# Expert stage of a decoder layer: a fixed TensorE order with neighbouring pairs of experts interleaved

## The chip, the cores and the metric

The kernel runs on one core of a Trainium2 chip, as one program. The metric is the device time in microseconds (us) from one launch, lower is better. All data are float32 in HBM; weights alone are about 460 MB, of which the experts' are 403 MB.

## The reference

One decoder layer over 256 tokens of width 1024: a token-mixing part with four gated branches, a layer norm, then a sparse expert layer and a second norm. The change concerns the expert layer (cut to what matters; `EXPERT_BLOCK` padding left out):

```
logits = h @ w_router + b_router                # 32 experts
top_v, top_e = top_k(logits, 4); gates = softmax(top_v)
for each expert e, for its tokens xb:
    hdn = xb @ w_up[e] + b_up[e]                # 1024 -> 2048
    glu = min(hdn[..., ::2], 7); lin = clip(hdn[..., 1::2], -7, 7)
    act = glu * sigmoid(1.702 * glu) * (lin + 1)
    y[token] += gate * (act @ w_down[e] + b_down[e])   # 1024 -> 1024
h = layer_norm(alpha * h + y)
```

Every expert is used by some tokens, so all of w_up (8.39 MB an expert) and w_down (4.19 MB) is read once.

## The kernel before

**Slabs and the stream of weights.** SBUF is an arena of 25 slabs, each 128 partitions by 2048 floats (1 MB). Weights and working buffers take slabs from it. All weight pieces stand in one list in the order of their use (`specs`); `load_one` (L267) takes a slab and issues the next load on SP's queue, and `pump(reserve)` issues loads while more than `reserve` slabs are free. A slab is reused when its last reader has ended, so a load waits in SP's queue for the engine that last used its slab. In the expert stage two slabs are kept free (`RES_MOE`), and nine from the last but one pair on (`RES_OVER`), for the overflow pass. A piece of w_up is 128 rows of 2048 floats: one 8 KB row for each partition. A piece of w_down is 256 rows of 1024 floats, as two 4 KB rows for each partition, row `p` and row `128 + p` (`rows`).

**Pairs of experts.** The experts are taken two at a time, in 16 pairs (`for e0`, L1592). Each expert has 64 places for tokens. `gather` (L1355 to L1364) builds the selection of the two experts' tokens on VectorE and GpSimd, multiplies the 256 tokens by it on TensorE into two PSUM tiles (pxs, L1360), and ScalarE writes the 8 pieces of transposed rows with the norm's gain and offset (L1364). `pair` (L1398) then does:

- the up product: 8 chunks of rows k, each with two slabs (one an expert); for each of four column blocks nb and both experts one matmul of 128 rows, 64 columns of the array and 512 values (L1416) into one of four PSUM tiles hp. The two experts of a pair use different halves of the array's columns. The biases are added by a matmul (L1410);
- `places`: the transposed selection and the gates of the places (L1437, L1439), copied by ScalarE (L1441);
- `hidden`: the activation of each of the four column blocks, one operation on ScalarE (L1424) and four on VectorE (L1423 to L1427), and two transposes on TensorE (pta, L1429), copied back by ScalarE (L1515);
- the down product: 4 chunks of two slabs, 8 matmuls each (L1447) into two PSUM tiles dp;
- in the third pair (`RESID`), the scaled residual, the output biases and the largest count of tokens of any expert (`residual`, L1368);
- `scatter`: the result times the gates in two float32r parts (ScalarE L1452, VectorE L1453), back to the tokens by matmuls (psc, L1456, L1457), added to the sum of all pairs on VectorE (L1463).

**The last pair** has its weights cut by columns, in the order `LAST`, so that w_up's blocks and w_down's halves alternate; these pieces have rows of 2 KB. Its result is added to the sum in PSUM (yf, L1478), and the second norm follows (L1618 on).

**The overflow pass.** An expert with more than 64 tokens would need a second pass. `overflow` (L1543) reads the largest count into a register of every engine (L1545) and branches around the pass (L1546); with these inputs the pass is not run. It stands ahead of the last pair. Behind it two loads go to ScalarE's queue (`OTHER`).

**What sets the order.** Within a dependency order, a scheduler of the language orders each engine's instructions by its own estimates of costs. The kernel writes the matmuls of a chunk with the experts alternating; the scheduler may move them. It also decides where the next pair's gather or the residual's matmuls stand among the others.

PSUM has 8 banks: four of tag pp (hp, yf), two of pt (pxs, psg, pta, psc and others), two of pd (dp).

Of the kernel before, what the change touches and what calls it, by code (L numbers as in the profile page):

```python
# [23 lines left out]
T = 256  # L24
# [31 lines left out]
OTHER = 2  # L56
ROWS_AT = 3
RES_OVER = 9
# [86 lines left out]
class Part:  # L145
    """A piece of a block that is freed as a whole."""
# [28 lines left out]
def tile_trunk(ctx, tc, a, out):  # L175
# [71 lines left out]
    # The last pair's weights come in an order that leaves little to do when the last of them is there: w_up by blocks  # L247
    # of columns, w_down by halves of its columns, the chunks of the first half as soon as their rows can be used.
# [64 lines left out]
            # ScalarE rounds; VectorE, and GpSimd for the last quarter, take the rest  # L313
# [20 lines left out]
    class Half:  # L334
        """Half of the columns of a tile that was split as a whole."""
# [31 lines left out]
    class X:  # L367
        """An activation [128, k, T] in two float32r parts."""
# [5 lines left out]
        def split(self, sl, src, hi_src=None, eng=None):  # L374
            """src: float32 on SBUF or PSUM"""
# [47 lines left out]
    class Moments:  # L423
        """Mean and reciprocal deviation over D, by halves."""
# [61 lines left out]
    # small parameters of the scan  # L486
# [115 lines left out]
        # a - 1 = expm1(x) cos(t) - 2 sin^2(t/2) + i a_im; divided by lam  # L602
# [41 lines left out]
        # the same with the halves exchanged: [im; re]  # L644
# [10 lines left out]
    def turn(dst, src, sine, sign):  # L655
        """The sine's part of a rotation of the pairs [re; im]: the halves change places."""
# [4 lines left out]
    def scan_part(m):  # L661
        """S5: the tables of eight groups, then V, the scan over chunks, and the outputs."""
# [6 lines left out]
        # E[state, g, k, n] = a^k b_bar ; Cp[state, g, k, n] = c a^(k+1)  # L669
# [15 lines left out]
        # taps k[n', (tau, n)] with seven zero taps before them, laid out in DRAM  # L685
# [61 lines left out]
    def scan_in():  # L747
        """S5 inputs by chunks of eight steps, the latest step first."""
# [19 lines left out]
    def scan_out():  # L768
# [17 lines left out]
        # gelu, tanh form  # L786
# [13 lines left out]
    def select():  # L800
        """Indexer scores and the best 64 keys of every query."""
# [39 lines left out]
    def sparse():  # L841
        """Attention over the selected latents."""
# [61 lines left out]
    def memory():  # L904
        """Attention over the memory."""
# [38 lines left out]
    # -- main stream: one weight tile after the other ------------------------  # L944
# [13 lines left out]
    def main():  # L958
# [21 lines left out]
        # residual in token layout  # L980
# [11 lines left out]
        # indexer and latents  # L992
# [60 lines left out]
        # convolution  # L1053
# [26 lines left out]
        # gates and branches: twice the merged value, transposed  # L1080
# [57 lines left out]
    def rows_in():  # L1138
        """Parameters of the experts: b_up in two stacked float32r parts, b_down and the norms' rows below it."""
# [17 lines left out]
    def route_in():  # L1157
        """The router's weights times the norm's gain, their sums, and what the norm's offset adds to the bias."""
# [82 lines left out]
    # -- output projection, first norm, router, by blocks of 128 tokens --------  # L1241
    # The router's product is taken before the norm: its gain rides on the weights, mean and deviation on the result.
# [58 lines left out]
    for b in range(2):  # L1301
# [20 lines left out]
        # places from 1 on, 0 for an expert that is not chosen  # L1322
# [5 lines left out]
    def gates():  # L1328
# [21 lines left out]
    def gather(sl):  # L1350
        """Rows of two experts, transposed; sl: their slots, [128, 2, 2]."""
        S2, xs = B(128, 2, 2, CAP), B(128, KC, 2 * CAP)
        for b in range(2):
            for e in range(2):
                (V if b else G).tensor_scalar(S2.ap[:, b, e, :], slot_i, sl[:, b, e:e + 1], None, op0=OP.is_equal)  # L1355
        p = [PT("pxs") for _ in range(2)]
        for b in range(2):
            for k in range(KC):
                # one flag for the groups of a bank
                PE.matmul(p[k // 4][:, k % 4 * 128:(k % 4 + 1) * 128], hN.ap[:, b, k * 128:(k + 1) * 128],  # L1360
                          S2.ap[:, b].rearrange("p e s -> p (e s)"), start=b == 0 and k % 4 == 0, stop=b == 1,
                          skip_group_check=True)
        for k in range(KC):
            S.activation(xs.ap[:, k, :], p[k // 4][:, k % 4 * 128:(k % 4 + 1) * 128], AF.Identity, bias=col(3, k),  # L1364
                         scale=col(2, k))
        return xs, S2

    def residual():  # L1368
        """The scaled residual and the output biases; the largest count."""
# [28 lines left out]
    def pair(xs, S2, gt, up_k, dn_k, pick, mid=None, first=False, last=None):  # L1398
# [20 lines left out]
        def hidden(nb, p):  # L1419
            """The activation of a block, transposed."""  # L1420
            hv = hp[nb].rearrange("p (f two) -> p f two", two=2)
            g, l, t = B(128, 256), B(128, 256), B(128, 256)
            V.tensor_scalar(g.ap, hv[:, :, 0], LIMIT, None, op0=OP.min)  # L1423
            S.activation(t.ap, g.ap, AF.Tanh, scale=0.5 * SWA)  # L1424
            V.tensor_scalar(l.ap, hv[:, :, 1], LIMIT, -LIMIT, op0=OP.min, op1=OP.max)
            V.scalar_tensor_tensor(l.ap, l.ap, 1.0, g.ap, op0=OP.add, op1=OP.mult)
            V.scalar_tensor_tensor(l.ap, t.ap, 1.0, l.ap, op0=OP.add, op1=OP.mult)  # L1427
            for j in range(2):
                PE.transpose(p[:, j * 128:(j + 1) * 128], l.ap[:, j * 128:(j + 1) * 128], ident)  # L1429
# [3 lines left out]
        def places():  # L1433
            """The transposed selection and the half gates of the slots."""
# [15 lines left out]
        def scatter(nb):  # L1450
            sl = slice(nb * 512, (nb + 1) * 512)
            S.activation(r_(yh.ap[:, sl]), dp[nb], AF.Copy, scale=gs_)  # L1452
            V.scalar_tensor_tensor(r_(yl.ap[:, sl]), dp[nb], gs_, yh.ap[:, sl], op0=OP.mult, op1=OP.subtract)  # L1453
            for b in range(2):
# [10 lines left out]
        if last:  # L1465
# [3 lines left out]
            yh, yl = R(128, D), R(128, D)  # L1469
            for what, j, k0, kn in LAST:  # L1470
# [4 lines left out]
                if what == DOWN and k0 == 0:  # L1475
# [17 lines left out]
                if what == DOWN and k0 + kn == KC:  # L1493
                    scatter(j)
        else:
# [13 lines left out]
            aT, ST = B(128, KC, 128), R(128, 2, 128)  # L1509
            gs_ = places()  # L1510
            for n2 in range(2):
                p = PT("pta")
                for i in range(2):
                    hidden(2 * n2 + i, p[:, i * 256:(i + 1) * 256])
                S.copy(aT.ap[:, n2 * 4:n2 * 4 + 4, :].rearrange("p k c -> p (k c)"), p)  # L1515
            dp = [PD(f"dp{i}") for i in range(2)]
            for k2 in range(KC // 2):
                with dn_k(k2) as wd:
                    for i, nb, e in ((i, nb, e) for i in range(2) for nb in range(2) for e in range(2)):
                        down(nb, 2 * k2 + i, e, wd[e][:, i, nb * 512:(nb + 1) * 512])  # L1520
            if mid:
# [4 lines left out]
            for nb in range(2):  # L1526
                scatter(nb)
        for t in (aT, ST, yh, yl):
            t.free()
# [13 lines left out]
    def overflow():  # L1543
        """Tokens past an expert's first 64."""
        cnt = nc.values_load(cnt_i[0:1, 0:1], min_val=0, max_val=T)  # L1545
        with tc.If(cnt > CAP):  # L1546
# [26 lines left out]
            with tc.For_i(0, T // CAP - 1, 1):  # L1573
                V.tensor_scalar(far, far, -float(CAP), None, op0=OP.add)
                with tc.For_i(0, NE, 2) as e0:
# [3 lines left out]
                    xs, S2 = gather(sl.ap)  # L1579
                    pair(xs.ap, S2.ap, gt.ap,  # L1580
# [67 lines left out]
```

## Time and profile before

| what | value |
|---|---|
| median of 3 runs | 1433.44 us (1432.83 to 1434.91) |
| span of the profiled execution | 1434.6 us |
| mean granted TensorE clock | 0.964 |
| bytes read by the weight queue | 454.80 MB in 133520 packets |
| loads of w_up on SP's queue | 255 of 1024 KB, 9.9 us from issue to landing |
| loads of w_down on SP's queue | 123 of 1024 KB (9.3 us) and 9 of 512 KB (7.3 us) |
| first expert matmul | 409.5 us |

How to read the lines: `L1416` is a line of the kernel; `PE` is a TensorE matmul, `PEld` its weight load, `DVE` VectorE, `ACT` ScalarE, `POOL` GpSimd, and a `q` behind a name means the engine's instruction queue (`SPq` issues loads). `hp<-slab,slab x112` means 112 such records that write tile hp. A float32 matmul has two records. In brackets stands the idle time before, and what ended it.

### The profile page before, as it was taken

How to read it: one execution, taken by the hardware profiler on the slowest of the kernel's cores; microseconds unless marked ns; L12 is line 12 of the kernel's file. 1: busy time of each engine (PE TensorE's matmuls, PEld its weight loads, DVE VectorE, ACT ScalarE, POOL GpSimd, SP SyncE). 2: the span in 40 equal slices, each digit the busy share in tenths (PEclk: the TensorE clock that was granted, in tenths of full speed). 3: DMA queues.
4: the chain of work that ended last, by engine and by line, in shares of the span. 5: the costliest groups of instructions: out<-in, count | busy, mean ns of one | idle time of the engine just before them, and what ended most of it. 6: DMA issues, size and time to landing. Idle time of an engine off the chain costs nothing. (4 is left out here: it accounts for less than half of the span.)

```text
span 1434.6 us, 17340 instructions
## 1 busy us (share of the span) xinstructions
PE 1332.6 (93%) x6936; PEld 722.8 (50%) x6936; DVE 472.4 (33%) x972; ACT 315.0 (22%) x600; POOL 162.7 (11%) x190
## 2 busy tenths in 40 slices
PE   8898889999999999999999999999999999999896
PEld 8697889899953343334243343434333343433332
DVE  5797935755623113311203111120211112021113
ACT  5553333654322010101101010110101011010101
POOL 3124341446210000000000000000000000000000
PEclk9899988999999999999999999999999999999898
DMA  9524155884799999699999999999999999999390
GB/s 262 216 63 129 60 158 177 267 322 181 292 347 418 384 423 427 262 427 398 396 394 410 395 398 427 398 395 402 390 405 380 426 394 426 399 401 385 119 336 30
DMA packets 137046, 463.38 MB, mean 323 GB/s; under 512 B 19352, under 2 KB 54240, under 8 KB 105952
## 3 DMA queue, kind: packets, MB, share of 16 engines
q1 hardware_dynamic: 133520, 454.80, 80.2%
q0 software_dynamic: 2608, 5.83, 1.6%
q10 hardware_dynamic: 832, 1.58, 0.3%
q8 instruction: 57, 0.93, 0.2%
q14 instruction: 29, 0.24, 0.0%
HBM read 459.09 MB, written 3.08 MB: 322 GB/s over the span
## 5 line engine op out<-in xcount | busy, mean ns | idle before, releaser
L1416 PE MATMUL hp<-slab,slab 128*64 128x512 f32 x2048 | 524.1, 599 | 0.0
L1416 PEld LDWEIGHTS hp<-slab,slab 128*64 128x64 f32 x2048 | 179.4, 137 | 309.8 <-issue 307.4
L1447 PE MATMUL dp<-slab,slab 128*64 128x512 f32 x1024 | 266.0, 625 | 10.1 <-ACT slab L1515 10.1
L1447 PEld LDWEIGHTS dp<-slab,slab 128*64 128x64 f32 x1024 | 77.3, 142 | 158.6 <-issue 141.8
L323 DVE TENSOR_TENSOR slab<-slab,slab 128x1024 fp32r<-128x1024 f32 (+1 forms) x90 | 105.1, 1178 | 60.3 <-ACT slab L318 54.5
L1355 POOL TENSOR_SCALAR slab<-slot_i,slot 128x64 f32<-128x64 f32 x32 | 14.0, 452 | 942.1 <-PE psg L1439 780.1
L318 ACT CAST slab<-slab 128x1024 fp32r<-128x1024 f32 x90 | 92.7, 1049 | 69.5 <-issue 13.6
L323 POOL TENSOR_TENSOR slab<-slab,slab 128x256 fp32r<-128x256 f32 (+1 forms) x58 | 90.6, 1567 | 149.0 <-ACT slab L318 123.2
L1441 ACT CAST slab<-psg 128x256 fp32r<-128x256 f32 x16 | 6.0, 373 | 357.5 <-PE hp L1410 354.9
L384 PE MATMUL pg<-slab,slab 128*128 128x256 f32 x256 | 75.4, 295 | 0.0
L386 PE MATMUL pg<-slab,slab 128*128 128x256 f32 x256 | 75.4, 294 | 0.0
L1355 DVE TENSOR_SCALAR slab<-slot_i,slot 128x64 f32<-128x64 f32 x32 | 7.0, 254 | 205.1 <-PE psg L1439 198.0
L385 PE MATMUL pg<-slab,slab 128*128 128x256 f32 x256 | 74.4, 291 | 0.0
L1360 PE MATMUL pxs<-slab,slab 128*128 128x128 f32 x512 | 63.6, 284 | 5.7 <-DVE slab L1463 4.3
L1364 ACT ACTIVATE slab<-pxs,pcol 128x128 f32<-128x128 f32 x128 | 46.5, 468 | 102.3 <-PE pxs L1360 102.3
L1360 PEld LDWEIGHTS pxs<-slab,slab 128*128 128x128 f32 x512 | 60.6, 197 | 12.1 <-issue 10.3
L1423 DVE TENSOR_SCALAR slab<-hp 128x256 f32<-128x256 f32 x64 | 26.8, 419 | 98.1 <-PE hp L1416 90.9
L1424 ACT ACTIVATE slab<-slab 128x256 f32<-128x256 f32 x64 | 26.7, 417 | 140.1 <-DVE slab L1423 140.1
L1429 PE MATMUL pta<-ident,slab 128*128 128x128 f32 x128 | 29.8, 316 | 24.4 <-DVE slab L1427 23.0
L384 PEld LDWEIGHTS pg<-slab,slab 128*128 128x128 f32 x256 | 50.6, 198 | 1.9 <-issue 1.4
L386 PEld LDWEIGHTS pg<-slab,slab 128*128 128x128 f32 x256 | 50.7, 198 | 0.9 <-issue 0.9
L385 PEld LDWEIGHTS pg<-slab,slab 128*128 128x128 f32 x256 | 50.6, 198 | 0.9 <-issue 0.9
(449 smaller groups left out, 1592.7 us busy)
## 6 DMA issues: line engine op xcount, KB each, us to landing
slab<-in_w_up_dram SPq DMA_DIRECT2D x255, 1024.0 KB, 9.9
slab<-in_w_down_dram SPq DMA_DIRECT2D x123, 1024.0 KB, 9.3
slab<-in_w_in_dram SPq DMA_DIRECT2D x29, 1024.0 KB, 6.2
slab<-in_w_branch_dram SPq DMA_DIRECT2D x8, 1024.0 KB, 6.3
slab<-in_w_down_dram SPq DMA_DIRECT2D x9, 512.0 KB, 7.3
slab<-in_w_mem_kv_dram SPq DMA_DIRECT2D x4, 1024.0 KB, 11.2
slab<-in_w_o_dram SPq DMA_DIRECT2D x4, 1024.0 KB, 7.1
slab<-kp_d POOLq DMA_DIRECT2D x32, 64.0 KB, 3.3
```

The source lines that it names most:

```text
L318: ins = S.copy(r_(hi[:, sl]), src[:, sl])
L323: ins = eng.tensor_tensor(r_(lo[:, p0:p1]), src[:, p0:p1], hi[:, p0:p1], op=OP.subtract)
L384: PE.matmul(dst, lh, rh, start=first, stop=False)
L385: PE.matmul(dst, lh, rl, start=False, stop=False)
L386: PE.matmul(dst, ll, rh, start=False, stop=last)
L1360: PE.matmul(p[k // 4][:, k % 4 * 128:(k % 4 + 1) * 128], hN.ap[:, b, k * 128:(k + 1) * 128], S2.ap[:, b].rearrange("p e s -> p (e s)"), st ...
L1364: S.activation(xs.ap[:, k, :], p[k // 4][:, k % 4 * 128:(k % 4 + 1) * 128], AF.Identity, bias=col(3, k), scale=col(2, k))
L1416: PE.matmul(hp[nb][e * 64:(e + 1) * 64, :], xs[:, k, e * CAP:(e + 1) * CAP], w, start=start, stop=k == KC - 1, skip_group_check=True)
L1423: V.tensor_scalar(g.ap, hv[:, :, 0], LIMIT, None, op0=OP.min)
L1424: S.activation(t.ap, g.ap, AF.Tanh, scale=0.5 * SWA)
L1429: PE.transpose(p[:, j * 128:(j + 1) * 128], l.ap[:, j * 128:(j + 1) * 128], ident)
L1447: PE.matmul(dp[nb][e * 64:(e + 1) * 64, :], aT.ap[:, k, e * 64:(e + 1) * 64], w, start=k == 0, stop=k == KC - 1, skip_group_check=True)
```

## The change

1. **A fixed order on TensorE.** The expert stage stands in `manual_schedule` for TensorE: its instructions run in the order in which the kernel writes them. The other engines' are ordered by the scheduler as before. In each chunk the two experts' matmuls alternate.
2. **Neighbouring pairs interleaved.** The gather of the next pair begins with the pair (selection), its matmuls are split into two halves, behind the chunk before the last and behind the last of the up product. `places` moves behind chunk 3 (`PLACES_AT`). The first two blocks of `hidden` stand ahead of the down product, the third and fourth behind its first and second chunk. The scaling by the gates (`shares`) stays at the end of a pair, but the matmuls of the scatter are returned as a function (`add`) and run behind the first chunk of the next pair's up product (`behind`).
3. **w_down by two rows a partition.** A piece of 256 rows is laid out with rows `2p` and `2p + 1` in partition p, one run of 8 KB. `hidden` therefore takes the activation's columns in another order (`p (q i two) -> p i q two`), in the overflow pass in the old one.
4. **The overflow pass inside the last pair**, ahead of the third piece of w_down's first half (`OVER_AT`). The reservation of nine slabs and the two loads on ScalarE's queue go.

The rest of the difference is comments. The core of the diff:

```diff
-OTHER = 2
+OVER_AT = (0, 4)
+PLACES_AT = 3
-RES_OVER = 9
...
-            specs.append((src.rearrange("(i p) c -> p i c", p=128), (i, src.shape[1])))
+            specs.append((src.rearrange("(p i) c -> p i c", p=128), (i, src.shape[1])))
...
+    class Gather:
...
+        def half(self, h):
+            p = PT("pxs")
+            for b in range(2):
+                for i in range(4):
+                    k = 4 * h + i
+                    PE.matmul(p[:, i * 128:(i + 1) * 128], hN.ap[:, b, k * 128:(k + 1) * 128],
+                              self.S2.ap[:, b].rearrange("p e s -> p (e s)"), start=b == 0 and i == 0, stop=b == 1,
+                              skip_group_check=True)
+            for i in range(4):
+                k = 4 * h + i
+                S.activation(self.xs.ap[:, k, :], p[:, i * 128:(i + 1) * 128], AF.Identity, bias=col(3, k),
+                             scale=col(2, k))
...
         def hidden(nb, p):
-            hv = hp[nb].rearrange("p (f two) -> p f two", two=2)
-            g, l, t = B(128, 256), B(128, 256), B(128, 256)
+            hv = hp[nb].rearrange("p (q i two) -> p i q two", i=2, two=2) if paired else \
+                hp[nb].rearrange("p (i q two) -> p i q two", i=2, two=2)
+            g, l, t = B(128, 2, 128), B(128, 2, 128), B(128, 2, 128)
...
         if last:
...
+            behind()
             for what, j, k0, kn in LAST:
...
+                if what == DOWN and (j, k0) == OVER_AT:
+                    over()
-                if what == DOWN and k0 == 0:
+                if what == DOWN and (j, k0) in (OVER_AT, (1, 0)):
                     for b in range(2):
                         last[b].y[j] = P("yf")
...
                 if what == DOWN and k0 + kn == KC:
+                    shares(j)
                     scatter(j)
...
         else:
...
+                if k == 0 and behind:
+                    behind()
+                if k == PLACES_AT:
+                    aT, ST = B(128, KC, 128), R(128, 2, 128)
+                    gs_ = places()
+                if k == KC - 2 and ahead_:
+                    ahead_.half(0)
+            if ahead_:
+                ahead_.half(1)
+            ga.free()
+            for nb in range(2):
+                p = PT("pta")
+                hidden(nb, p)
+                S.copy(aT.ap[:, 2 * nb:2 * nb + 2, :].rearrange("p k c -> p (k c)"), p[:, :256])
...
             for k2 in range(KC // 2):
                 with dn_k(k2) as wd:
                     for i, nb, e in ((i, nb, e) for i in range(2) for nb in range(2) for e in range(2)):
                         down(nb, 2 * k2 + i, e, wd[e][:, i, nb * 512:(nb + 1) * 512])
+                if k2 < 2:
+                    nb = 2 + k2
+                    p = PT("pta")
+                    hidden(nb, p)
+                    S.copy(aT.ap[:, 2 * nb:2 * nb + 2, :].rearrange("p k c -> p (k c)"), p[:, :256])
...
+            for nb in range(2):
+                shares(nb)
+
+            def add():
+                for nb in range(2):
+                    scatter(nb)
+                for t in (ST, yh, yl):
+                    t.free()
+            return add
...
-    for e0 in range(0, NE, 2):
-        final = e0 == NE - 2
-        if e0 == NE - 4:
-            st["spare"] = RES_OVER
-        if final:
-            overflow()
-            st["spare"] = RES_MOE
-        xs, S2 = gather(slot[:, :, e0:e0 + 2])
...
-            for _ in range(OTHER):
-                tc.keep_in_program_order(load_one(nc.scalar))
...
+    ga, behind = Gather(slot[:, :, 0:2]).all(), None
+    gates()
+    with tc.manual_schedule(engines={mybir.EngineType.PE}):
+        for e0 in range(0, NE, 2):
+            final = e0 == NE - 2
+            after = None if final else Gather(slot[:, :, e0 + 2:e0 + 4])
...
+            behind = pair(ga, gh[:, :, e0:e0 + 2],
...
+                          residual if e0 == RESID else None, e0 == 0, ln2 if final else None, after, behind, not final,
+                          overflow)
+            ga = after
```

More of the change, by code (lines that the diff above doesn't have):

```diff
@@ L1348, in vec_row, with __init__, all, free @@
         return p
[L1350 to L1366, printed above, removed]
+    class Gather:
+        def __init__(self, sl):
+            self.S2, self.xs = B(128, 2, 2, CAP), B(128, KC, 2 * CAP)
+            for b in range(2):
+                for e in range(2):
+                    (V if b else G).tensor_scalar(self.S2.ap[:, b, e, :], slot_i, sl[:, b, e:e + 1], None,
+                                                  op0=OP.is_equal)
+        def half(self, h):
+            p = PT("pxs")
+            for b in range(2):
+                for i in range(4):
[7 more added lines that the diff above has]
+                             scale=col(2, k))
+        def all(self):
+            for h in range(2):
+                self.half(h)
+            return self
+        def free(self):
+            for t in (self.xs, self.S2):
+                t.free()
     def residual():
@@ L1396, in residual, with pair @@
         V.tensor_copy(cnt_i, cf)
-    def pair(xs, S2, gt, up_k, dn_k, pick, mid=None, first=False, last=None):
+    def pair(ga, gt, up_k, dn_k, pick, mid=None, first=False, last=None, ahead_=None, behind=None, paired=True,
+             over=None):
+        xs, S2 = ga.xs.ap, ga.S2.ap
         hp = {}
@@ L1428, in hidden @@
             for j in range(2):
-                PE.transpose(p[:, j * 128:(j + 1) * 128], l.ap[:, j * 128:(j + 1) * 128], ident)
+                PE.transpose(p[:, j * 128:(j + 1) * 128], l.ap[:, j, :], ident)
             for q in (g, l, t):
@@ L1448, in down, with shares @@
                       stop=k == KC - 1, skip_group_check=True)
-        def scatter(nb):
+        def shares(nb):
             sl = slice(nb * 512, (nb + 1) * 512)
@@ L1453, in scatter @@
             V.scalar_tensor_tensor(r_(yl.ap[:, sl]), dp[nb], gs_, yh.ap[:, sl], op0=OP.mult, op1=OP.subtract)
+        def scatter(nb):
+            sl = slice(nb * 512, (nb + 1) * 512)
             for b in range(2):
@@ L1493, in pair @@
                 if what == DOWN and k0 + kn == KC:
+                    shares(j)
                     scatter(j)
+            for t in (aT, ST, yh, yl):
+                t.free()
+            ga.free()
         else:
@@ L1508, in pair @@
                             up(nb, k, e, wu[e][:, nb * 512:(nb + 1) * 512], k == 0)
-            aT, ST = B(128, KC, 128), R(128, 2, 128)
-            gs_ = places()
-            for n2 in range(2):
+                if k == 0 and behind:
[7 more added lines that the diff above has]
+                ahead_.half(1)
+            ga.free()
+            for nb in range(2):
                 p = PT("pta")
[L1513 to L1516, printed above, removed]
+                hidden(nb, p)
+                S.copy(aT.ap[:, 2 * nb:2 * nb + 2, :].rearrange("p k c -> p (k c)"), p[:, :256])
+            dp = [PD(f"dp{i}") for i in range(2)] if paired else [P(f"dp{i}") for i in range(2)]
             for k2 in range(KC // 2):
@@ L1520, in pair @@
                         down(nb, 2 * k2 + i, e, wd[e][:, i, nb * 512:(nb + 1) * 512])
+                if k2 < 2:
[3 more added lines that the diff above has]
+                    S.copy(aT.ap[:, 2 * nb:2 * nb + 2, :].rearrange("p k c -> p (k c)"), p[:, :256])
+            aT.free()
             if mid:
@@ L1526, in pair @@
             for nb in range(2):
-                scatter(nb)
-        for t in (aT, ST, yh, yl):
-            t.free()
+                shares(nb)
[3 more added lines that the diff above has]
+                for t in (ST, yh, yl):
+                    t.free()
+            return add
     class Stream:
@@ L1578, in overflow @@
                     V.tensor_copy(pk.ap, id2[:, ds(e0, 2)])
-                    xs, S2 = gather(sl.ap)
-                    pair(xs.ap, S2.ap, gt.ap,
+                    pair(Gather(sl.ap).all(), gt.ap,
                          lambda k: Again([w_up[ds(e0 + e, 1), k * 128:(k + 1) * 128, :] for e in range(2)], 1),
                          lambda k2: Again([w_down[ds(e0 + e, 1), k2 * 256:(k2 + 1) * 256, :] for e in range(2)], 2),
-                         lambda e: pk.ap[:, e:e + 1])
-                    for t in (xs, S2):
-                        t.free()
+                         lambda e: pk.ap[:, e:e + 1], paired=False)()
             for t in (*wbufs, sl, gt, pk):
@@ L1591, in tile_trunk @@
     ln2 = [Moments(f"ln2{b}") for b in range(2)]
[L1592 to L1616 removed]
+    ga, behind = Gather(slot[:, :, 0:2]).all(), None
[4 more added lines that the diff above has]
+            after = None if final else Gather(slot[:, :, e0 + 2:e0 + 4])
+            if final:
+                gb2 = B(128, 2, D)
+                for i in range(2):
+                    for c in range(2):
+                        S.copy(gb2.ap[:, i, c * 512:(c + 1) * 512], vec_row(2 + i, c, PT("pbc")))
+            behind = pair(ga, gh[:, :, e0:e0 + 2],
+                          lambda k: Stream([ID_UP[e0, k], ID_UP[e0 + 1, k]]),
+                          lambda k2: Stream([ID_DN[e0, k2], ID_DN[e0 + 1, k2]]),
+                          lambda e: id2[:, e0 + e:e0 + e + 1],
+                          residual if e0 == RESID else None, e0 == 0, ln2 if final else None, after, behind, not final,
+                          overflow)
+            ga = after
     mv2, r2, nm2 = keep.tile([128, 2, 2], FT, name="mv2"), small([128, 2], "r2", 1), small([128, 2], "nm2", 1)
```

18 lines of the change are left out of this document (2 added, 16 removed).

## The prediction

> **What bounds the kernel now.** I read the page first, then the waits of the load queue (SP) and of TensorE (PE) in the expert stage, then windows over the transfers, then TensorE's order of time in single pairs, and last the chain that ends the run.
>
> ```profile
> span 1434.6 us, 17340 instructions
> ...
> PE 1332.6 (93%) x6936; PEld 722.8 (50%) x6936; DVE 472.4 (33%) x972; ACT 315.0 (22%) x600; POOL 162.7 (11%) x190
> ```
>
> TensorE is busy for 93% of the span, and a row of windows below has the transfers at 0.94 of theirs in the expert stage: two resources look full at once. They are told apart by who waits for whom. First the longest entry of what the load queue waited for between 610 and 1300 us (total, times, longest), then what TensorE waited for most in the same eleven pairs:
>
> ```profile
> SPq L267 <- PE hp L1416: 392.9, 154, 10.8
> ```
>
> ```profile
> PE pta L1429 <- DVE slab L1427: 16.5, 11, 1.5
> PE psc L1456 <- DVE slab L1463: 8.9, 11, 0.8
> PE dp L1447 <- ACT slab L1515: 7.4, 11, 0.7
> ```
>
> The loads wait for TensorE to hand back slabs. TensorE never waits for a load: its waits are for VectorE and ScalarE, 32.8 us in eleven pairs, 3.0 us a pair. So TensorE sets the pace, and the transfers follow it. How far behind their own limit are they? (Columns: window, length, busy time and count of PE, PEld, DVE, ACT, POOL, granted clock, DMA share, GB/s.)
>
> ```profile
> 438.20:1399.00 960.80, 902.43 (x3796) 351.87 (x3796) 182.89 (x447) 117.78 (x270) 13.08 (x30) 0.97 0.94 385
> 576.00:604.00 28.00, 25.77 (x116) 11.07 (x114) 9.88 (x18) 4.64 (x11) 0.00 (x0) 1.00 0.60 222
> 697.00:703.00 6.00, 6.00 (x13) 1.22 (x13) 2.11 (x6) 0.52 (x2) 0.00 (x0) 0.50 1.00 425
> 703.00:707.00 4.00, 4.00 (x22) 1.51 (x22) 0.00 (x0) 0.59 (x1) 0.00 (x0) 1.00 0.54 160
> 717.00:725.00 8.00, 6.85 (x47) 4.97 (x48) 2.76 (x7) 2.66 (x8) 0.00 (x0) 1.00 1.02 420
> 741.00:753.00 12.00, 12.00 (x53) 4.57 (x50) 0.00 (x0) 0.17 (x1) 0.00 (x0) 1.00 1.02 429
> 1218.00:1281.10 63.10, 59.30 (x254) 23.58 (x255) 12.59 (x31) 7.39 (x17) 0.85 (x2) 1.00 0.99 410
> 1300.00:1312.00 12.00, 12.00 (x57) 4.85 (x54) 0.00 (x0) 0.00 (x0) 0.00 (x0) 1.00 1.04 410
> 1324.00:1372.00 48.00, 41.37 (x154) 17.63 (x153) 6.49 (x16) 7.99 (x17) 0.96 (x2) 0.82 0.40 139
> ```
>
> Not far. With loads queued, w_up moves at 425 to 429 GB/s, w_down at 420, the last pair's narrow pieces at 410. In between the transfers stand still (160 GB/s from 703 to 707) because no slab is free. I take 427 GB/s as the limit for 8 KB rows and 409 for the last pair. A pair is 2 x (8.39 + 4.19) = 25.17 MB by its shapes, so 58.9 us at the limit. What TensorE needs is read from its order of time:
>
> ```profile
> 461.27 3.81 PE L1360 MATMUL pxs<-slab,slab 128*128 128x128 f32 x32 [0.29 <-ACT slab L1461]
> 465.01 24.25 PE L1416 MATMUL hp<-slab,slab 128*64 128x512 f32 x112
> ...
> 518.61 3.81 PE L1360 MATMUL pxs<-slab,slab 128*128 128x128 f32 x32 [0.33 <-DVE slab L1463]
> ...
> 593.47 3.81 PE L1360 MATMUL pxs<-slab,slab 128*128 128x128 f32 x32 [0.33 <-DVE slab L1463]
> ...
> 719.39 3.81 PE L1360 MATMUL pxs<-slab,slab 128*128 128x128 f32 x32 [0.34 <-DVE slab L1463]
> 723.13 12.29 PE L1416 MATMUL hp<-slab,slab 128*64 128x512 f32 x48
> ...
> 736.06 16.06 PE L1416 MATMUL hp<-slab,slab 128*64 128x512 f32 x64
> ```
>
> A matmul here fills 64 of the 128 columns and has two records; two experts' matmuls run side by side if they alternate. In pair 1 they do: 24.25 us for 112 records, 217 ns each, and the pair lasts 518.61 - 461.27 = 57.3 us. Later pairs take (719.39 - 593.47) / 2 = 63.0 us, and their records 256 and 251 ns: the scheduler has put one expert's matmuls in a row there. Pair 2, with the residual after its down product, takes 74.9 us, 12 more than the others.
>
> **The change, part by part.**
>
> *Alternating order and interleaved pairs.* Pair 1 shows the price of the first alone: 57.3 us instead of 63.0. On top of it the next pair's gather moves into the end of the up product, the scatter behind the next pair's first chunk, the third and fourth blocks of the hidden layer behind the first two down chunks. No operation is added; these moves remove waits. The comparisons that build the gather's selection (VectorE, GpSimd) are issued a pair earlier; both engines are mostly idle (33% and 11% busy). The 3.0 us of waits above were exposed because TensorE had nothing else in order. The scatter's operands will be ready after the first chunk, the hidden blocks while a down chunk runs. I leave 0.7 us of the waits (the second block waits for a PSUM buffer that the gather's second half still holds) and take out another 1 us of clock dips: 54 us a pair, with 52 and 57.3 as bounds. A pair that takes less than 58.9 us is set by its transfers.
>
> *The transfers, then.* From 438.2 us to the last weights' landing, where I end the window (1399), the core read 385 GB/s x 960.8 us = 369.9 MB. Without a standstill the first 344.7 MB take 807 us at 427 and the last pair's 25.2 MB take 61.5 us at 409: they would end at 1306.7. So the standstills are 92.3 us. Of these the stretch around the overflow pass holds 48 x (1 - 139/409) = 31.7 us, the residual's 28 x (1 - 222/427) = 13.4 us, and the other thirteen pairs the rest, 3.6 us each (the row of 703 to 707 alone has 4 x (1 - 160/427) = 2.5). What remains of them: the stock of loaded slabs is full when the stage begins, and one more slab is held by the next pair's gathered rows, so the first two pairs and the residual, now behind the down product in a fixed order, still stop the queue. I keep 10 us, between 0 and 28 (13.4 plus four pairs' 3.6). Later TensorE has used the stock up, and its pauses are absorbed. The transfers end at 1317.
>
> [...]
>
> *w_down by two rows a partition.* Packets of 4 KB become 8 KB, the shape of w_up. The row of pure w_down has 420 GB/s against 427: 8.39 MB gain 0.33 us a pair, 5 us in fifteen, counted above by using 427 throughout. If it brings nothing, those 5 us come back. VectorE now reads PSUM at twice the stride, with as many elements; I take that as free (a whole chain of four costs 1.8 us and lies beside matmuls), and a doubling would expose at most 1.8 us twice a pair, still within 57.3.
>
> *Overflow pass inside the last pair.* Today nine slabs are kept free for it and SP drains its loads before the branch: the 31.7 us. Now the reservation is gone and all loads stand in the queue before the branch, so the transfers go on through it. The two loads that ScalarE issued behind the branch join SP's queue in the same order, which costs SP two issues and nobody a wait. Behind the branch SP has only the four stores left to issue, so its drain delays none of the loads. TensorE still pays. The rows around the branch, and those of the last pair:
>
> ```profile
> 1340.43 0.73 PE L1456 MATMUL psc<-slab,slab 128*128 128x512 f32 x2
> ...
> 1343.60 0.40 PE L1457 MATMUL psc<-slab,slab 128*128 128x512 f32 x1
> 1349.77 0.76 PE L1410 MATMUL hp<-slab 64*128 64x512 f32 x1 [5.78 <-PEq L1546]
> ```
>
> ```profile
> 1318.16 0.42 DVE L1423 TENSOR_SCALAR slab<-hp 128x256 f32<-128x256 f32 x1 [2.88 <-PE hp L1416]
> ...
> 1319.96 0.44 PE L1429 MATMUL pta<-ident,slab 128*128 128x128 f32 x2
> ```
>
> ```profile
> 1350.53 5.90 PE pxs L1360 x32
> ...
> 1419.39 0.02 issue
> 1419.42 0.70 ACT slab L1452
> 1420.12 0.03 issue
> 1420.14 0.76 DVE slab L1453
> ```
>
> The last pair before runs from 1349.77 to 1419.39 on TensorE, 69.6 us. New: less the gather (5.9), plus the scatter of the pair before (1340.43 to 1344.00, 3.6), plus the branch (1349.77 - 1343.60 = 6.2), plus, in a fixed order, four waits of 1.8 us for the hidden blocks (7.2, from 1318.16 to 1319.96), the first half's scatter waiting 1.5 for ScalarE and VectorE (0.70 + 0.76), 1 for the last chunk, where one expert's matmuls follow the other's, less 3 for the clock (0.82 in 1324 to 1372). Sum 80.2 us, between 70 and 87. This exceeds the 61.5 us of its transfers, so TensorE sets the end here.
>
> *Sum.* The last pair's TensorE work begins when the pair before has landed, 61.5 us before 1317, plus 4.5 for landing and its last chunk (16 records x 217 ns = 3.5): 1260. Plus 80.2: 1340.2. Plus the norm and the stores, untouched, 1434.6 - 1419.4 = 15.2: a span of 1355.4. The profiled execution is 1.2 us above the median of the runs, so 1354.2, rounded to **1354 us**, 5.5% less. By TensorE alone the end would be at 461.3 + 14 P + 12 + 80.2 + 15.2 = 569 + 14 P, with P the length of a pair: 1325 for 54. TensorE takes over from P = 56.2.
>
> **The rivals.**
>
> *TensorE stays the bound.* In a fixed order every wait is exposed, and another instruction can't be put into it. For it: the three kinds of wait above. Against it: they are 3.0 us a pair in all. With P of 58 to 60 the end is 1381 to 1409.
>
> *The limit isn't sustained.* 425 to 429 GB/s are windows of 6 to 12 us; the longest row without a large hole is a whole pair at 410. At 410 the 344.7 MB take 841 us, 34 more: 1389. The DMA share of 0.99 in that row speaks for it, the holes of 3.6 us a pair against it.
>
> *The clock falls when TensorE waits for loads (slower).* The granted clock is 0.50 in the window 697 to 703, after pair 4's waits for VectorE, and 0.82 around the branch; now TensorE would wait in every pair. About 49 of the 54 us scale with the clock, so at a mean of 0.86 P is 62 and the end 1437: below that the change loses; at 0.80, P = 66 and 1493. Against it: a slower TensorE waits less, and the mean was 0.97 with waits in every pair. [...]
>
> *The order isn't what it says.* Were the two experts' matmuls still in rows, 63 us a pair would stay, and only the overflow's 31.7 us less the 10 it costs in the last pair would go: 1412.
>
> **How the numbers follow.** Forecast 0.73, TensorE-bound 0.13, lower limit 0.06, no effect of the order 0.04, clock 0.04. The range runs from 1334 (no standstill left, 10 us less, and a last pair of 70 us, 10 less) up to 1398 (P = 59.2, the lower limit inside it); outside lie the worst of the TensorE-bound case, the clock and the order. About 0.2%, 3 us, is what a measurement of this kernel can tell from no change. Faster 0.94, within 0.2% 0.02, slower 0.04.
>
> **What would show it.** In the changed profile: the load queue's waits for TensorE nearly gone after the fourth pair and waits of TensorE for loads in their place; 420 GB/s or more in the slices of the expert stage, with no hole near the end; records of 217 ns in every pair; pairs of about 55 us at first and 58.9 later; w_down windows at 427; a pause of about 6 us on TensorE at the branch, some 50 us before the end. Wrong would be: pairs over 60 us with loads still waiting for slabs (TensorE-bound), no waiting on either side at 410 GB/s (the limit), or a granted clock well below 0.97.

## The result and the profile after

The changed kernel takes 1367.8 us (median of 4 runs, 1364.5 to 1372.2), the kernel before beside it 1433.1 us (median of 4): a ratio of 0.9554, 95% interval 0.9504 to 0.9604. So the change makes it 4.5% faster, 65 us, where 5.5% was forecast. The line numbers of the changed kernel differ: the up product is now L1436, the down product L1468, the transposes of the hidden layer L1450, the scatter L1481 and L1482, the loads L268.

The page of the changed kernel: its span and the busy time of the engines, then the transfers in GB/s in 40 equal slices, and how long a load of w_up takes to land.

```profile
span 1370.4 us, 17361 instructions
...
PE 1250.6 (91%) x6936; PEld 694.3 (51%) x6936; DVE 474.3 (35%) x972; ACT 318.1 (23%) x630; POOL 166.7 (12%) x190
...
GB/s 265 236 63 115 85 116 139 269 292 277 158 361 345 315 426 427 427 355 428 427 426 426 427 427 426 426 427 427 425 427 426 427 427 427 427 427 425 407 312 31
...
slab<-in_w_up_dram SPq DMA_DIRECT2D x256, 1024.0 KB, 19.6
```

The same 6936 matmul records take 1250.6 us of TensorE instead of 1332.6. From the 19th to the 37th slice the transfers stand at 425 to 428 GB/s with no hole. Two dents are left ahead of them: the 13th and 14th slice (345 and 315), the first pair, and the 18th (355), the pair with the residual. The landing of a load takes 19.6 us instead of 9.9, because loads now queue behind loads. The waits of the load queue say the same (changed kernel; total us, times, longest): two entries between 620 and 890 us, then the same two between 890 and 1230 us.

```profile
SPq L268 <- DMA slab<-in_w_up_dram: 108.3, 54, 3.4
...
SPq L268 <- PE hp L1436: 38.1, 17, 5.5
...
SPq L268 <- DMA slab<-in_w_up_dram: 187.0, 90, 3.4
...
SPq L268 <- PE hp L1436: 4.3, 15, 0.4
```

Before, the queue's largest entry was TensorE (392.9 us). Now it is the queue's own earlier loads, and from 890 us on, the ninth pair, the queue hardly waits for TensorE any more (4.3 us in 340). The prediction had expected that after the fourth pair. On the other side, what TensorE waits for between 640 and 1230 us:

```profile
PE pta L1450 <- ACT slab L1554: 16.0, 10, 1.6
PE hp L1436 <- DMA slab<-in_w_up_dram: 15.9, 18, 1.2
PE psc L1481 <- DVE slab L1488: 4.5, 11, 0.4
```

It waits for weights, which it did not in the eleven pairs of before, and 1.6 + 0.4 us in every pair for ScalarE and VectorE. The pairs can be timed by the first instruction of `places`, which stands in each at the same point of the fixed order (changed kernel, TensorE in order of time):

```profile
666.95 0.44 PE L1458 MATMUL psg<-ident,slab 128*128 128x128 f32 x2
...
879.67 0.44 PE L1458 MATMUL psg<-ident,slab 128*128 128x128 f32 x2
...
1173.87 0.44 PE L1458 MATMUL psg<-ident,slab 128*128 128x128 f32 x2
...
1232.80 0.44 PE L1458 MATMUL psg<-ident,slab 128*128 128x128 f32 x2
...
1272.89 3.97 PE L1347 MATMUL pbc<-slab,ident 4*128 4x512 f32 x8
...
1331.96 1.19 PE L1506 MATMUL yf<-slab,ident 128*128 128x512 f32 x1 [6.43 <-PEq L1596]
1334.95 2.72 PE L1506 MATMUL yf<-slab,ident 128*128 128x512 f32 x3 [1.80 <-issue]
...
1346.33 8.85 PE L1468 MATMUL dp<-slab,slab 128*64 128x512 f32 x32
```

From 666.95 to 879.67 lie four pairs, 53.2 us each; from 1173.87 to 1232.80 one of 58.9. The first is TensorE's own pace, the second is 25.17 MB at 427 GB/s (the experiments below bear this out). The last pair runs from 1272.89 to the end of the last down matmul (1346.33 + 8.85 = 1355.18), 82.3 us, and the norm and the stores take 15.2 us, as before.

The windows over the transfers of the changed kernel (columns as in the prediction) show where the rate was lost:

```profile
438.20:620.00 181.80, 166.07 (x734) 62.56 (x736) 45.05 (x100) 26.57 (x63) 2.99 (x6) 0.92 0.95 392
...
620.00:1228.00 608.00, 570.38 (x2705) 227.93 (x2702) 125.33 (x306) 83.21 (x208) 11.23 (x22) 1.00 1.01 427
...
438.20:1330.00 891.80, 820.98 (x3808) 322.02 (x3808) 189.12 (x456) 123.14 (x303) 14.23 (x28) 0.98 1.00 417
```

Over 608 us nothing is lost: 427 GB/s throughout. In the 181.8 us from 438.2 on, 181.8 x (1 - 392/427) = 14.9 us are.

### The profile page after: what moved, and what is told of

Its sections match the earlier page's. It is cut to its first block, busy times and chain, and to the rows that moved or that the text cites. A ratio compares the mean times of both kernels' runs of the same rounds, so it can differ in the third digit from the quotient of the medians.

```text
span 1370.4 us, 17361 instructions
## 1 busy us (share of the span) xinstructions
PE 1250.6 (91%) x6936; PEld 694.3 (51%) x6936; DVE 474.3 (35%) x972; ACT 318.1 (23%) x630; POOL 166.7 (12%) x190
## 5 line engine op out<-in xcount | busy, mean ns | idle before, releaser
L1436 PE MATMUL hp<-slab,slab 128*64 128x512 f32 x2048 | 476.2, 600 | 18.2 <-DMA slab<-in_w_up_dram 18.2
L1436 PEld LDWEIGHTS hp<-slab,slab 128*64 128x64 f32 x2048 | 155.9, 138 | 304.6 <-issue 251.3
L1468 PE MATMUL dp<-slab,slab 128*64 128x512 f32 x1024 | 233.2, 599 | 0.0
L1468 PEld LDWEIGHTS dp<-slab,slab 128*64 128x64 f32 x1024 | 70.0, 137 | 130.2 <-issue 130.2
L1427 DVE CAST slab<-id 128x64 fp32r<-128x64 f32 x38 | 5.6, 192 | 193.3 <-PE hp L1430 187.9
L1450 PE MATMUL pta<-ident,slab 128*128 128x128 f32 x128 | 26.7, 290 | 31.6 <-ACT slab L1554 24.0
L1488 DVE TENSOR_TENSOR slab<-slab,psc 128x512 f32<-128x512 f32 x56 | 36.2, 684 | 36.2 <-PE psc L1482 36.1
## 6 DMA issues: line engine op xcount, KB each, us to landing
slab<-in_w_up_dram SPq DMA_DIRECT2D x256, 1024.0 KB, 19.6
```

Source lines behind the costliest of these rows:

```text
L1436: PE.matmul(hp[nb][e * 64:(e + 1) * 64, :], xs[:, k, e * CAP:(e + 1) * CAP], w, start=start, stop=k == KC - 1, skip_group_check=True)
L1450: PE.transpose(p[:, j * 128:(j + 1) * 128], l.ap[:, j, :], ident)
L1468: PE.matmul(dp[nb][e * 64:(e + 1) * 64, :], aT.ap[:, k, e * 64:(e + 1) * 64], w, start=k == 0, stop=k == KC - 1, skip_group_check=True)
L1488: V.tensor_tensor(yacc[0].ap[:, b, sl], yacc[0].ap[:, b, sl], p, op=OP.add)
```

## The experiments

The theory was: the fixed order and the interleave together take TensorE's pair from 63 to 53 us, below the transfers' 58.9; then transfers set the pace, and first and last pair are TensorE's. The rivals: one part alone does it (the order, the 8 KB rows, or the overflow pass's place, to which the prediction's sum had credited 31.7 us).

**w_down as before, all else changed.**

```diff
-            specs.append((src.rearrange("(p i) c -> p i c", p=128), (i, src.shape[1])))
+            specs.append((src.rearrange("(i p) c -> p i c", p=128), (i, src.shape[1])))
```

(with `hidden`'s columns as before). 

> The changed kernel with the old rows of w_down (two 4 KB rows a partition). Theory, transfers set the pace of the later pairs: w_down moves at 420 instead of 427 GB/s, 0.33 us a pair, 5 us in all (3 to 8), about 1373 us against 1368 for the changed kernel. Rival, the packets of 4 KB were themselves the cause of the holes in the transfers: holes come back in each pair, 1380 us or more.

Measured 1371.6 us, 0.9585 (0.9523 to 0.9647). The sign and size fit the theory, but the interval overlaps the changed kernel's. The rate shows it more sharply: between 620 and 900 us this kernel moves

```profile
620.00:900.00 280.00, 267.97 (x1315) 106.73 (x1312) 59.31 (x147) 40.28 (x101) 5.07 (x10) 1.00 1.02 424
```

where the changed one has 427. That is 0.4 us a pair. No holes came back, so the rival, packets of 4 KB as their cause, is out.

**The overflow pass ahead of the last pair again**, with nine slabs kept free.

```diff
-                if what == DOWN and (j, k0) == OVER_AT:
-                    over()
...
+            if e0 == NE - 4:
+                st["spare"] = RES_OVER
+            if final:
+                overflow()
+                st["spare"] = RES_MOE
```

> The changed kernel with the overflow pass ahead of the last pair again and nine slabs kept free for it. Theory: SP drains its loads and stands still around the branch, 15 to 30 us of transfers are lost and the last pair waits for them, 1383 to 1398 us. Rival, the place is immaterial because TensorE pays its 6 us at the branch either way: 1368 within 5 us.

Measured 1366.2 us, 0.955 (0.9481 to 0.9619). The theory fell: the place of the pass makes no difference that the runs can tell. The hole in the transfers is there (its windows), 12 x (1 - 203/409) = 6.0 us in this row, less than the 15 to 30 expected:

```profile
1280.00:1292.00 12.00, 11.01 (x32) 4.17 (x33) 3.57 (x10) 0.37 (x1) 0.00 (x0) 0.63 0.56 203
```

But the last pair is TensorE's: its matmuls wait for no load in it. They begin at the same time (1273.25, behind the branch), and the branch stops TensorE for less at this place (its order of time):

```profile
1273.25 5.54 PE L1348 MATMUL pbc<-slab,ident 4*128 4x512 f32 x8 [2.80 <-DVEq L1595]
...
1340.94 8.86 PE L1469 MATMUL dp<-slab,slab 128*64 128x512 f32 x32
```

2.80 us ahead of the pair, against 6.43 + 1.80 inside it; from 1273.25 to 1349.80 the pair lasts 76.5 us instead of 82.3, or 79.3 with the 2.80 counted in. The hole costs nothing, since the transfers do not end this kernel.

**The interleaved kernel without the fixed order.**

```diff
-    with tc.manual_schedule(engines={mybir.EngineType.PE}):
+    if True:
```

> The changed kernel without the fixed TensorE order: the interleaving stays as written, but the scheduler may move the matmuls. Theory, the alternation of the experts is lost without the fixed order: pairs of 60 us or more, records over 240 ns in the up product, 1400 to 1425 us. Rival, the written interleaving alone removes the waits and the order is kept well enough: 1365 to 1378 us.

Measured 1471.8 us, 1.0281 (1.0211 to 1.0351): slower than before the change. The direction is the theory's, the size larger than its 1400 to 1425. The chunks of the up product show why (that kernel, TensorE in order of time):

```profile
734.49 5.42 PE L1436 MATMUL hp<-slab,slab 128*64 128x512 f32 x16
...
749.15 16.06 PE L1436 MATMUL hp<-slab,slab 128*64 128x512 f32 x64
...
799.89 0.44 PE L1458 MATMUL psg<-ident,slab 128*128 128x128 f32 x2 [0.25 <-DVE slab L1488]
...
865.99 0.44 PE L1458 MATMUL psg<-ident,slab 128*128 128x128 f32 x2 [0.25 <-DVE slab L1488]
```

339 ns a record in a chunk that the scheduler has cut off by a piece of gather or scatter, 251 elsewhere, 217 nowhere in these rows. So the up product is no faster than in the later pairs of before (256 and 251); that the experts stand in rows again is inferred from this, since the rows do not name the expert. The pair lasts 865.99 - 799.89 = 66.1 us.

**The fixed order alone**, in the kernel before, without any interleave.

```diff
-    for e0 in range(0, NE, 2):
-        final = e0 == NE - 2
+    with tc.manual_schedule(engines={mybir.EngineType.PE}):
+        for e0 in range(0, NE, 2):
+            final = e0 == NE - 2
```

> The kernel before with nothing changed but the fixed TensorE order over the expert stage: gather, up product, hidden blocks, down product and scatter one after the other, experts alternating. Theory, the pairing of the experts' matmuls is the larger part of the gain: pairs of 57 to 58.9 us, the residual in one piece, 1378 to 1395 us. Rival, in a fixed order without interleaving every wait is exposed and eats the gain: pairs of 60 us or more, 1405 us or more.

Measured 1422.4 us, 0.9941 (0.9906 to 0.9976). The rival was right: alone, the order brings 0.6%, less than 2% and just clear of the noise. Its order of time, one pair:

```profile
720.53 3.81 PE L1360 MATMUL pxs<-slab,slab 128*128 128x128 f32 x32 [0.35 <-DVE slab L1463]
724.27 24.25 PE L1416 MATMUL hp<-slab,slab 128*64 128x512 f32 x112
...
755.49 0.61 PE L1429 MATMUL pta<-ident,slab 128*128 128x128 f32 x2 [1.73 <-DVE slab L1427]
757.61 0.69 PE L1429 MATMUL pta<-ident,slab 128*128 128x128 f32 x2 [1.51 <-DVE slab L1427]
759.80 0.69 PE L1429 MATMUL pta<-ident,slab 128*128 128x128 f32 x2 [1.50 <-DVE slab L1427]
760.42 16.63 PE L1447 MATMUL dp<-slab,slab 128*64 128x512 f32 x64
...
780.91 3.81 PE L1360 MATMUL pxs<-slab,slab 128*128 128x128 f32 x32 [0.34 <-DVE slab L1463]
```

The up product has its 217 ns, but the waits for the hidden blocks stand open, 1.73 + 1.51 + 1.50 us, and then the down product is slow: 260 ns a record. The clock tells why:

```profile
757.00:761.00 4.00, 1.89 (x6) 0.87 (x8) 2.05 (x6) 0.93 (x3) 0.00 (x0) 0.50 1.01 426
761.00:765.00 4.00, 4.00 (x12) 1.19 (x10) 0.00 (x0) 0.11 (x1) 0.00 (x0) 0.50 1.01 426
```

The granted clock is halved from the three waits into the down product. The pair takes 780.91 - 720.53 = 60.4 us, and the mean clock of the run is 0.927. This is close to the prediction's "clock" rival, with waits for VectorE in place of waits for loads. The interleave keeps it out: the changed kernel's clock is 1.00 from 620 to 1228 us.

**The rows of w_down alone**, in the kernel before: only the `(i p)` to `(p i)` of the first diff, with the columns to match.

> The kernel before with w_down by two rows a partition, and the hidden layer's columns to match, nothing else. Theory, TensorE sets the pace there, so faster transfers only wait longer for slabs: within 0.3% of the kernel before. Rival, the 4 KB packets are part of what makes the holes: 0.5% or more faster.

Measured 1430.7 us, 0.999 (0.9952 to 1.0028), as the theory had it. The run is weak evidence by itself: the 5 us that the rows could bring at most by the prediction's sum are 0.35%, inside this interval.

**Half of w_down left out of the changed kernel's loads**, and the other half used twice, so that TensorE has the same work.

```diff
+            specs.append((src[:128].rearrange("(p i) c -> p i c", p=128), (1, src.shape[1])) if src.shape[0] == 256 else
+                         (src.rearrange("(p i) c -> p i c", p=128), (i, src.shape[1])))
```

> The changed kernel with half of w_down left out in all but the last pair: each piece loads 128 rows of 256 and uses them twice, so the output is not the reference's; TensorE's work is the same. Transfers are 21.0 MB a pair, 49 us. Theory, transfers set the pairs from the eighth on: these stay at 53.2 us, and the end comes at 1334 (1326 to 1342). Rival, TensorE sets all pairs and the 58.9 us are its own: 1368 within 5.

Measured 1327.6 us, 0.927 (0.9215 to 0.9325). Now the late pairs last 53.2 us too (two of them in order of time):

```profile
1087.68 0.44 PE L1459 MATMUL psg<-ident,slab 128*128 128x128 f32 x2
...
1140.86 0.44 PE L1459 MATMUL psg<-ident,slab 128*128 128x128 f32 x2
```

The same TensorE work with fewer bytes is 40 us shorter, so 53.2 us is TensorE's own pace, and from the ninth pair on (879.67 us) the changed kernel is bound by its transfers.

**The overflow pass and its branch left out.**

```diff
-                if what == DOWN and (j, k0) == OVER_AT:
-                    over()
```

> The changed kernel with the overflow pass and its branch left out (the tokens past the first 64 of an expert would be lost; with these inputs there are none). Theory, TensorE sets the last pair, not its transfers: the 6.4 us at the branch and the 1.8 us behind it go, 1358 to 1362 us. Rival, the transfers' end sets the end: 1365 us or more.

Measured 1357.3 us, 0.9496 (0.9432 to 0.9559), 10 us less and just below the theory's range; none of its runs (1355.3 to 1360.5) reaches the changed kernel's (from 1363.8 up). The last pair is TensorE's: the same weights come, and a pause less on TensorE ends the run earlier.

What was left was the 14 us by which the changed kernel missed the forecast. Two places were suspected, the first pairs and the last.

**The bias rows fetched earlier.** In the first pair TensorE stops (changed kernel, order of time):

```profile
435.37 2.05 PE L1367 MATMUL pxs<-slab,slab 128*128 128x128 f32 x16
441.23 0.82 PE L1430 MATMUL hp<-slab 64*128 64x512 f32 x2 [3.80 <-DVE slab L1153]
442.48 1.22 PE L1430 MATMUL hp<-slab 64*128 64x512 f32 x2 [0.43 <-DVE slab L1153]
443.62 6.08 PE L1436 MATMUL hp<-slab,slab 128*64 128x512 f32 x16
```

```profile
444.00:448.00 4.00, 4.00 (x12) 0.98 (x10) 2.00 (x6) 0.54 (x2) 0.00 (x0) 0.50 0.57 242
```

It waits for the output of L1153, the split of the bias rows in two float32r parts, and then runs at half the clock (380 ns a record; the window has 0.50). The bias rows are fetched at chunk 3 (`ROWS_AT`).

```diff
-ROWS_AT = 3
+ROWS_AT = 1
```

> The changed kernel with the experts' bias rows fetched behind the first chunk of the first pair instead of the third (ROWS_AT = 1). Theory, the 5.5 us in which TensorE waits for them in the first pair, and with it the loads at 444 to 452 us, go; what the transfers gain there is kept to the end: 3 to 6 us less, 1362 to 1365. Rival, TensorE has slack later and the transfers make it up: no difference within 2 us.

Measured 1371.2 us, 0.9565 (0.9508 to 0.9622): no gain. The wait of 3.80 us stays. It isn't the fetch: the split's first operation stands on ScalarE behind the gather's (changed kernel, ScalarE in order of time):

```profile
437.51 1.51 ACT L1372 ACTIVATE slab<-pxs,pcol 128x128 f32<-128x128 f32 x4 [12.11 <-PE pxs L1367]
438.90 2.09 ACT L1152 CAST slab<-slab 32x1024 fp32r<-32x1024 f32 x2
```

**The split itself earlier, and the residual in the ninth pair.**

```diff
-ROWS_AT = 3
-RESID = 4
+SPLIT_AT = 5
+ROWS_AT = 1
+RESID = 16
...
+                if first and k == SPLIT_AT:
+                    rows_split()
                 if k == KC - 1:
-                    if first:
-                        rows_split()
```

> The changed kernel with the two steps moved that stop TensorE early in the stage: the bias rows are split behind chunk 4 of the first pair's up product instead of chunk 6 (ahead of the gather's copies on ScalarE), and the residual stands in the ninth pair (RESID = 16) instead of the third. Theory, both stops hit a full stock of slabs and cost transfers, 8 us at 444 to 460 and 5 us at 596 to 612; later TensorE has slack: 8 to 13 us less, 1355 to 1360 us, transfers of 427 GB/s without a hole from 470 us on. Rival, the stops are made up later anyway: 1368 within 3.

Measured 1355.7 us, 0.9478 (0.9441 to 0.9515): 12 us less than the changed kernel beside it (1367.4, below), within the theory's range; the two moves were not run apart. The window that lost 14.9 us now reads

```profile
438.20:620.00 181.80, 174.39 (x858) 68.08 (x855) 38.47 (x99) 30.37 (x75) 4.05 (x8) 1.00 1.01 426
```

**The last pair rearranged**: the transposes of a hidden block behind the piece that follows it, the last piece with the experts alternating, the norm's constant rows a pair earlier.

```diff
-                    if len(wd) > 2:
-                        order.sort(key=lambda o: o[1])
...
+                if pend:
+                    turned(*pend.pop())
                 if what == UP and k0 + kn == KC:
-                    p = PT("pta")
-                    hidden(j, p)
-                    S.copy(aT.ap[:, 2 * j:2 * j + 2, :].rearrange("p k c -> p (k c)"), p[:, :256])
+                    pend.append((j, activated(j)))
...
-            if final:
+            if e0 == NE - 4:
                 gb2 = B(128, 2, D)
```

> The changed kernel with three edits in the last pair alone: the transposes of a hidden block stand behind the next piece's matmuls, the last piece alternates the experts, and the norm's rows are spread (8 records, 4 us) a pair earlier, in TensorE's slack. Theory, TensorE sets the last pair (82 us against 61.5 us of transfers): 7.6 + 1.8 + 4.0 = 13 us less, 1352 to 1358 us. Rival, the transfers' end at 1328 sets it with what must follow: 1363 or more.

Measured 1359.8 us, 0.9497 (0.9458 to 0.9535): 7.7 us less than the changed kernel, between what theory and rival allowed, so neither number held. On TensorE the pair went from 82.3 to 71.7 us, 10.6 less (order of time of its first and last piece of work):

```profile
1271.97 0.44 PE L1466 MATMUL psg<-ident,slab 128*128 128x128 f32 x2
...
1336.60 7.09 PE L1476 MATMUL dp<-slab,slab 128*64 128x512 f32 x32
```

The last chunk has 222 ns a record instead of 277. What lies between 10.6 us of the profiled pair and 7.7 us of the medians is within the spread of the runs (1355.2 to 1362.2); nothing further is claimed for it. Of the 10.6, 4 us are the constant rows, which now stand in the pair before, and 3.1 come at the branch, which stops TensorE for 3.32 us there instead of 6.43; that was not reckoned with, and its cause stays open.

**Both together.** 

> The two before this one together. Theory, the two gains stand one behind the other and add up: 20 to 26 us less than the changed kernel, 1342 to 1348 us. Rival, with a shorter last pair the transfers' end takes over or the early gain was slack: no better than the better one of the two.

Measured 1346.4 us, 0.9403 (0.9366 to 0.944), the fastest kernel here that reads all weights: 21 us less than the changed one, about the sum of the two (12 and 8). In its last pair TensorE now waits for a piece of w_up (its order of time), so that the transfers are close behind there too:

```profile
1302.54 3.65 PE L1437 MATMUL hp<-slab,slab 128*64 128x512 f32 x14 [1.52 <-DMA slab<-in_w_up_dram]
...
1327.82 7.09 PE L1477 MATMUL dp<-slab,slab 128*64 128x512 f32 x32
```

**The changed kernel again**, beside the last three and on their chip. 

> The changed kernel itself beside the other three, on the same chip, so that they can be compared with it: 1368 within 4 us.

Measured 1367.4 us (1363.8 to 1369.7), 0.9558 (0.952 to 0.9595).

## Why the prediction was right, and where it was not

*What bounds the kernel before* was right: TensorE. Its load queue waits for TensorE and TensorE for no load, and faster rows alone change nothing that can be told (0.999).

*The pair on TensorE*, 54 us, measured 53.2; the waits left are 1.6 + 0.4 us a pair (0.7 was allowed, with 1 us for the clock). That the sum came so close has some luck in it. The prediction took 57.3 as the price of the alternation alone; alone it gives 60.4, for the waits and the clock that come with it. And it gave the interleave 3.3 us, where 60.4 to 53.2 is 7.2: two misses that cancel. Neither part is worth much without the other: -0.6% in time for the order, +2.8% for the interleave.

*The limit of the transfers*, 427 GB/s and 58.9 us a pair, was exact, over 608 us. The rival with 410 GB/s is out. A second core at work was not run.

*The standstills* are the term that was sized too small: "I keep 10 us" (with 0 to 28 as bounds). In the 181.8 us from 438.2 on alone 14.9 are lost, at two pauses of TensorE: about 9 from 438.2 to 470 us (307 GB/s) and about 6 from 575 to 620 us (373 GB/s). The first is the split of the bias rows (3.80 us and a half clock behind it), which the trace of before did not have. It comes from the interleave: the gather's copies now stand ahead of the split on ScalarE. In the kernel before the bias matmuls follow without a wait (433.72 us); with the interleave and no fixed order they wait 2.0 us. The second is the residual. Before, the scheduler spread its matmuls among the down product's; in a fixed order its chain of VectorE steps stands alone on TensorE, 20.3 us where the prediction had 12 for the pair (its three waits, 3.04, 2.23 and 1.29 us here, were 2.5, 2.2 and 1.3 with the order alone):

```profile
574.92 1.98 PE L1347 MATMUL pbc<-slab,ident 4*128 4x512 f32 x4
579.93 3.78 PE L1347 MATMUL pbc<-slab,ident 4*128 4x512 f32 x4 [3.04 <-DVE slab L1391]
585.94 0.61 PE L1398 MATMUL pgt<-ident,gn 128*32 128x128 f32 x2 [2.23 <-DVE slab L1391]
587.84 7.19 PE L1404 MATMUL pbd<-slab,slab 32*128 32x512 f32 x8 [1.29 <-ACT slab L1399]
...
595.26 5.36 PE L1436 MATMUL hp<-slab,slab 128*64 128x512 f32 x16
```

Besides, 417 GB/s x 891.8 us = 371.9 MB came after 438.2 us, 2.0 MB more than reckoned from before, 4.7 us; and the last loads trickle (167 GB/s from 1325.5 to 1331.9 us). With the 4.9 us of standstills that makes about 11: transfers end near 1328, not 1317, and the last pair starts at 1272.9, not 1260. Part of this is one execution against another: when the changed kernel ran again, its profile had 13.6 us lost in the same 181.8 (395 GB/s) and the last pair from 1267.5. The experiment that takes both pauses away gave 12 us back.

*The last pair*, 80.2 us, measured 82.3. The branch cost its 6.4 (6.2 foreseen), the four hidden waits 1.88 + 1.87 + 1.97 + 1.94 = 7.7 (7.2), the last chunk 1.8 (1), the scatter's wait 1.1 (1.5); the pause of 1.80 us behind the branch wasn't in the sum. Together with the later start: 12.9 + 2.1 = 15.0 us, the span of 1370.4 against 1355.4. In the second profile it is 7.5 + 1.8 = 9.3, a span of 1364.7.

*w_down's rows*: 5 us counted, 3 to 4 measured, at the edge of what the runs can tell.

*The overflow pass's place* was argued wrongly though the sum came out. The 31.7 us around it were counted as a loss of the transfers that the change would remove, and the rival "the order isn't what it says" was priced at 1412 by taking them as removable alone. Put back ahead of the changed kernel's last pair, the pass costs nothing. In the kernel before, moving the pass alone was not run. But its trace speaks for the same: between 1300 and 1425 us no matmul waits for a load, weight loads do for 0.4 us in all, and what TensorE pays is the branch's 5.78 us.

## What to carry to other kernels

A fixed order and an interleave belong together: the order keeps matmuls paired, and the interleave fills the waits that the order exposes; alone, the order was worth 0.6% here and the interleave less than nothing. The length of a hole in the transfers is no gain to be had where another engine ends last, as here in the last pair; look first whether that engine waits for a load behind the hole. After such a change look at the first rounds and the last, where the new bound isn't yet or no longer in force: here they held 21 us, beside the 65 that the change itself brought.

## What the runs showed of the hardware

The granted TensorE clock was halved where no single wait was long: with three of 1.5 to 1.7 us, and two transposes between each, it was 0.50 for the 8 us from 757 to 765 in the kernel with the order alone, though TensorE was busy for 1.89 us of the first four and all of the last four. One wait of 1.6 us a pair in the changed kernel left it at 1.00 (620 to 1228 us).

The branch around the pass that isn't run stopped TensorE for 6.43 us in the changed kernel, and one matmul later stood a pause of 1.80 more; in other places of the order the stop was 2.80 and 3.32 us. The queue of instructions (q8, 57 packets and 0.93 MB in the run, 16 KB each) has one packet right there (the transfers of the changed kernel between 1331.9 and 1336 us):

```profile
q8 instruction: 1, 0.02, 1.4%
```

That this packet is TensorE's, and the cause of the 1.80 us, was not shown. One more packet of that queue lies in the 6.43 us before (1325.5 to 1331.9 us), as the last loads come in; what those 6.43 us consist of stays open.
